# TensorE takes eight of the first sixteen modulation sums, and x goes to the head of the load queue

## The chip, the core and the metric

One core of a Trainium2 chip runs the whole program. Its engines are TensorE (PE in the rows; its weight loads PEld), VectorE (DVE), ScalarE (ACT), GpSimd (POOL) and SyncE (SP), each with a queue of its own that is worked off in order, and 16 DMA engines, which the queues of SP, ACT and POOL feed. The metric is the device time of one execution in microseconds.

## The reference

Two blocks on x of 256 tokens by 1024 features, in float32. The first has a gated delta-rule layer and a forgetting-attention layer, the second sliding-window attention, pooling, and a mixture that gathers expert rows. The change lies at the head of the first layer:

```python
cond = jax.nn.silu(c)
for i in range(DEPTH):
    mod = cond @ ada_w[i] + ada_b[i]
    shift, scale, gate = jnp.split(mod[:, None, :], 3, axis=-1)
    h = rmsnorm(x, norm_w[i]) * (1 + scale) + shift
    y = gdn_mixer(h, ...)            # i = 0: starts with proj = h @ w_in
    x = x + gate * y
```

Here `mod` has 3072 values a layer: 24 tiles of 128, where tiles 0 to 7 are the shift, 8 to 15 the scale and 16 to 23 the gate.

## The kernel before

Features lie on the 128 partitions in chunks of 128, so h is eight chunks of 128 by 256 tokens. `fm_steps` (L499 to L514) makes two chunks at a time: four transposes of the normed x (`xhat`) into a PSUM tile, then for each chunk ScalarE's pass (L511, with the modulation's scale `msc` and shift `mod` as columns) into the high part, VectorE's same pass (L512) into `xw`, and a difference (L513) for the low part. The matmuls of the dense layers take weights as high and low parts too, in three products of 256 columns (`dense_all`).

A modulation tile t is summed on VectorE (`ada`, L597 to L606): a row tile `raw` of 128 by 1024 weights, 512 KB, is loaded on SP's queue, multiplied with `silc` (silu of c, on every partition) and summed along the row (L604) into column t of `mod`. `rawp` has four `raw` buffers, and weights use them as well, so a load waits until the sum that read its buffer is done. `first` lists the sixteen tiles that h needs, pairs of scale and shift; `more(4)` issues four. `mod_scale` (L614) adds the bias and forms `msc` for two chunks a step, as soon as its four tiles are summed.

The order at the start is the code's order as the framework's scheduler keeps it on each engine: c, four row tiles, then x (L662), the identity and the small columns `pcol` on SP's queue; ScalarE squares x, `rstd` (L462 to L480) makes its norm by thirteen small VectorE steps, ScalarE writes `xhat` (L672), TensorE transposes. Between the third and fourth `fm_steps` stand ten dummy matmuls each (`WARM`, L688 to L690). The transfers share eight semaphores in turn, so each waits for the one eight before it.

Weights come in units: 512 KB of a matrix, loaded by `load` (L312) and taken apart by `cast` (L327 on ScalarE, L328 on VectorE), or used whole in f32 (`whole`). Units 0 and 1 are the first halves of the first two q and k columns, units 2 and 3 their second halves, used whole; unit 4 begins the next pair. `unit` hands out a unit in the order of `plan` and casts ahead. `gates` (through `small_proj`) needs all eight chunks as well, in products of 32 weight columns. From there on matmuls of all kinds follow one another to the expert part, whose gathers on GpSimd's queue fill the last half of the program.

Of the kernel before, what the change touches and what calls it, by code (L numbers as in the profile page):

```python
# [22 lines left out]
T = 256  # L23
D = 1024
# [39 lines left out]
for _n, _w in (("nw", 16), ("ab", 48), ("conv", 128), ("qn", 1), ("kn", 1), ("bq", 8),  # L64
               ("bk", 1), ("bga", 8), ("bgp", 8), ("ps", 4), ("anw", 1)):
    PO[_n] = _o
    _o += _w
# [47 lines left out]
def _pc(v, n):  # L115
    return np.ascontiguousarray(v.reshape(n, 128).T)


def prepare(a):
# [13 lines left out]
        _pc(b2[gp2:], 8), _pc(a["pool_scale_2"][0], 4),  # L133
        _pc(a["a_norm_w"][0], 1)], axis=1)
# [3 lines left out]
    ada = np.concatenate([a["ada_w"][0].T, a["ada_w"][1].T]).reshape(48, 128, D).transpose(1, 0, 2)  # L138
    sk = a["sub_keys_2"][0].transpose(3, 0, 1, 2).reshape(128, 16 * 128)
# [71 lines left out]
def build(nc, tc, ctx, I, out, dbg=None, stop=None):  # L211
# [8 lines left out]
    def transpose(o, i, e):  # L220
        M.t += math.prod(o.shape[1:]) * 2 / 2.4
        nc.tensor.transpose(o, i, e)  # L222

# [77 lines left out]
    raws, spare = {}, []  # L301
    trickle = [iter(())]

# [158 lines left out]
    def rstd(ss, n, e, name):  # L462
# [9 lines left out]
        for _ in range(3):  # L472
            if w == 1:
                V.tensor_scalar(z, y, y, x, op0=OP.mult, op1=OP.mult)
                V.tensor_scalar(y, z, 1.5, y, op0=OP.add, op1=OP.mult)
            else:
                V.tensor_tensor(z, y, y, op=OP.mult)
                V.tensor_tensor(z, z, x, op=OP.mult)
                V.scalar_tensor_tensor(y, z, 1.5, y, op0=OP.add, op1=OP.mult)
        return y  # L480
# [17 lines left out]

    def fm_steps(hi, lo, src, scale, bias, whole):  # L499

        for k0 in range(0, 8, 2):
            p = pss.tile([128, 2, T], F32, name="ps")
            for k in range(2):
                for b in range(2):
                    transpose(p[:, k, b * 128:(b + 1) * 128],
                                        src[b][:, (k0 + k) * 128:(k0 + k + 1) * 128], ident)
            v = whole[:, k0 % 4:k0 % 4 + 2]
# [86 lines left out]
    V.scalar_tensor_tensor(silc, silc, 1.0, c_row, op0=OP.add, op1=OP.mult)  # L594
    mod = cst.tile([128, 48], F32, name="mod")
    ada_done, ada_last = set(), []

    def ada(ts):

        for t in ts:  # L600
            w = rawp.tile([128, KU * CW], F32, name="raw", bufs=RAW_BUFS)
            nc.sync.dma_start(w, I["ada"][:, t, :])
            jk = act.tile([128, D], BF, name="jk", bufs=1)
            i = V.scalar_tensor_tensor(jk, w, 0.5, silc, op0=OP.mult, op1=OP.mult, accum_out=mod[:, t:t + 1])  # L604
            ada_last.append(i.ins)
            ada_done.add(t)  # L606
            yield

    def mod_cols(t, n):
# [44 lines left out]

    first = ada(t + 8 * i for t in range(8) for i in (1, 0))

    def more(n):
        for _ in range(n):
            next(first)

    more(4)
    nc.sync.dma_start(xs, I["x"].rearrange("(b p) d -> p b d", b=2))  # L662
    nc.sync.dma_start(const[:, 0:128], I["const"][:, 0:128])
    nc.sync.dma_start(pcol, I["pcol"])
    more(4)
    ssp = sums(1)
# [4 lines left out]
    for b in range(2):  # L671
        A.activation(xh0[b], xs[:, b], AF.Copy, scale=r0[:, b:b + 1])  # L672
    hi, lo = fm_tiles()
# [3 lines left out]
    hx = lambda kt: (hi[:, kt], lo[:, kt]) + ((xw[:, kt - 4],) if kt > 3 else ())  # L677
    next(ms)
    next(fm)
    more(4)  # L680
    next(ms)
    next(fm)
    cast(2, ahead=0)
    more(4)
# [1032 lines left out]
```

## Time and profile before

| | |
|---|---|
| median of 3 runs | 1396.33 us (1393.62 to 1399.25) |
| the profiled execution | 1398.01 us, its span 1396.2 us |
| busy: PE, DVE, ACT, POOL | 1233.9, 1017.3, 558.6, 306.5 us |
| mean granted clock of TensorE | 0.972 of full |
| chain that ended last, by engine | PE 49%, DMA 28%, DVE 12% |

The span runs from the first instruction to the last; 1.8 us of the execution lie outside it. A row of the timeline gives start and length in microseconds, the engine, the source line, and the operation as output<-inputs; x3 means that three alike follow one another, and the brackets hold the idle time ahead and what ended it. A matmul's record is longer than its step to the next one, since they overlap in the array. An f32 product that is not split is two records.

### The profile page before, as it was taken

What the parts mean: (1) busy time and instruction counts of PE and PEld (TensorE: products, weight loads), DVE (VectorE), ACT (ScalarE), POOL (GpSimd) and SP (SyncE); (2) the same over time, 40 slices, a digit from 0 to 9 for tenths busy, and PEclk for the clock granted to TensorE, in tenths of its full rate; (3) what the DMA queues carried; (4) which work ended last, traced back from release to release, by engine and by line L of the source; (5) the groups of instructions that cost most, each with busy time, mean ns of one, the idle gap of its engine ahead of it and who ended that gap; (6) DMA issues with size and microseconds to landing.
All of it is one profiled execution on the core that took longest, in us unless ns stands there. A gap on an engine that the chain in (4) does not pass through costs nothing.

```text
span 1396.2 us, 20024 instructions
## 1 busy us (share of the span) xinstructions
PE 1233.9 (88%) x6880; PEld 887.5 (64%) x6880; DVE 1017.3 (73%) x2670; ACT 558.6 (40%) x1313; POOL 306.5 (22%) x295
## 2 busy tenths in 40 slices
PE   1999999999899999999999999887778787877886
PEld 1888988989899988889986565333333333323332
DVE  6799988987876688775547657766777766767655
ACT  3357656574455555674213223222222221222211
POOL 0000000000000000000014434444343534444452
PEclk9999999999999999999999999999999989999899
DMA  8656464733454525335849999999999999999996
GB/s 302 200 159 203 137 182 138 224 93 120 123 171 146 167 85 197 116 98 173 278 178 421 423 389 366 423 425 422 424 424 424 412 424 424 419 420 427 404 423 254
DMA packets 72085, 392.39 MB, mean 281 GB/s; under 512 B 8112, under 2 KB 8624, under 8 KB 39472
## 3 DMA queue, kind: packets, MB, share of 16 engines
q0 software_dynamic: 37296, 268.45, 46.4%
q1 hardware_dynamic: 32960, 117.41, 26.5%
q10 hardware_dynamic: 1728, 5.24, 1.0%
q8 instruction: 55, 0.90, 0.3%
q14 instruction: 46, 0.38, 0.1%
HBM read 390.03 MB, written 1.05 MB: 280 GB/s over the span
## 4 chain that ended last, share of the span: by engine, by line
PE 49%; DMA 28%; DVE 12%; issue 5%; POOL 3%; ACT 2%; SPq 0%; POOLq 0%; DVEq 0%; ACTq 0%
PE pd L218 29%; DMA er<-uv,idx 22%; PE pacc L218 7%; PE ps L218 6%; DVE jk L1625 3%; POOL er L1622 3%; DMA raw<-awi 3%; PE ip L218 2%; DVE lo L328 2%; PE acc L218 2%; DMA er<-uv,i 1%; PE po L218 1%; PE ps L222 1%; DMA raw<-ada 1%; DVE jk L604 1%
## 5 line engine op out<-in xcount | busy, mean ns | idle before, releaser
L218 PE MATMUL pacc<-er,dg 128*128 128x512 f32 x1024 | 489.0, 631 | 106.8 <-ACT dg L1635 104.4
L1622 POOL DMA_INDIRECT er<-uv,idx x253 | 285.0, 1127 | 778.8 <-DVE oh L1572 427.6
L218 PEld LDWEIGHTS pacc<-er,dg 128*128 128x128 f32 x1024 | 200.0, 201 | 379.1 <-issue 220.7
L1625 DVE SCALAR_TENSOR_TENSOR jk<-er,xn 128x1024 bf16<-128x1024 f32 x256 | 312.4, 1220 | 151.1 <-DMA er<-uv,idx 150.2
L328 DVE TENSOR_TENSOR lo<-raw,hi 128x1024 fp32r<-128x1024 f32 x122 | 148.6, 1221 | 55.9 <-ACT hi L327 55.1
L1629 ACT ACTIVATE ge<-dots,r 128x2 f32<-128x2 f32 (+2 forms) x95 | 28.0, 295 | 384.9 <-DVE jk L1625 384.9
L327 ACT ACTIVATE hi<-raw 128x1024 fp32r<-128x1024 f32 x122 | 129.3, 1060 | 131.0 <-PE pd L218 82.8
L218 PE MATMUL pd<-fm,hi 128*128 128x256 f32 x784 | 153.4, 292 | 3.5 <-ACT hi L327 3.3
L218 PEld LDWEIGHTS pd<-fm,hi 128*128 128x128 f32 x784 | 123.6, 192 | 5.2 <-ACT hi L327 3.7
L218 PE MATMUL pd<-hi,fm 128*128 128x256 f32 (+1 forms) x608 | 117.3, 289 | 2.1 <-DVE fm L496 1.3
L218 PE MATMUL pd<-fm,lo 128*128 128x256 f32 x392 | 112.6, 287 | 0.0
L1635 ACT ACTIVATE dg<-const,ge 128x128 f32<-128x128 f32 x250 | 83.0, 391 | 37.3 <-DVE ge L1631 33.4
L218 PEld LDWEIGHTS pd<-hi,fm 128*128 128x128 f32 x608 | 95.5, 192 | 3.8 <-issue 2.3
L218 PE MATMUL pd<-lo,fm 128*128 128x256 f32 (+1 forms) x304 | 86.8, 287 | 1.6 <-DVE lo L328 1.6
L218 PEld LDWEIGHTS pd<-fm,lo 128*128 128x128 f32 x392 | 75.1, 192 | 0.2 <-issue 0.2
L218 PE MATMUL pd<-xw,raw 128*128 128x256 f32 x256 | 68.0, 391 | 2.9 <-DVE xw L512 1.7
L604 DVE SCALAR_TENSOR_TENSOR jk<-raw,silc 128x1024 bf16<-128x1024 f32 x48 | 58.5, 1219 | 2.9 <-DMA raw<-ada 2.6
L218 PEld LDWEIGHTS pd<-lo,fm 128*128 128x128 f32 x304 | 58.1, 192 | 2.0 <-DVE lo L328 2.0
L827 POOL TENSOR_SCALAR_AFFINE_SELECT am<-am 128x256 f32<-128x256 f32 x16 | 6.5, 406 | 213.0 <-DVE am L825 201.1
L873 ACT ACTIVATE is<-acc 128x256 f16<-128x256 f32 x96 | 36.9, 385 | 30.6 <-PE acc L218 28.7
L218 PEld LDWEIGHTS pd<-xw,raw 128*128 128x128 f32 x256 | 44.5, 193 | 7.0 <-DVE xw L512 2.0
L879 DVE TENSOR_TENSOR iy<-ip,fac 128x256 f16<-128x256 f32 x96 | 40.4, 420 | 9.0 <-PE ip L218 7.5
(393 smaller groups left out, 2151.9 us busy)
## 6 DMA issues: line engine op xcount, KB each, us to landing
raw<-ada SPq DMA_DIRECT2D x48, 512.0 KB, 4.4
raw<-awi SPq DMA_DIRECT2D x48, 512.0 KB, 4.1
raw<-bwi SPq DMA_DIRECT2D x32, 512.0 KB, 3.6
raw<-wi SPq DMA_DIRECT2D x30, 512.0 KB, 3.5
raw<-awo SPq DMA_DIRECT2D x16, 512.0 KB, 3.6
raw<-wqy SPq DMA_DIRECT2D x14, 512.0 KB, 7.7
raw<-bwo SPq DMA_DIRECT2D x8, 512.0 KB, 3.7
raw<-wau SPq DMA_DIRECT2D x8, 512.0 KB, 3.6
```

The source lines that it names most:

```text
L218: nc.tensor.matmul(o, l, r, **kw)
L222: nc.tensor.transpose(o, i, e)
L327: A.activation(hi, r3, AF.Copy)
L328: V.tensor_tensor(lo, r3, f(hi), op=OP.subtract)
L604: i = V.scalar_tensor_tensor(jk, w, 0.5, silc, op0=OP.mult, op1=OP.mult, accum_out=mod[:, t:t + 1])
L827: G.affine_select(am, am, pattern=[[0, 2], [1, 128]], base=0, channel_multiplier=-1, compare_op=OP.not_equal, fill=1.0)
L873: A.activation(s[:, 0:2], acc[:, 0:2], AF.Copy)
L879: V.tensor_tensor(y, p, bc2(FH[f"m{m}"]), op=OP.mult)
L1622: G.indirect_dma_start(out=r, out_offset=None, in_=I["uv"], in_offset=bass.IndirectOffsetOnAxis(ap=idx[:, b, h, s + i:s + i + 1], axis=0))
L1625: at["dot"] = V.scalar_tensor_tensor(jk, r[:, 0:D], 1.0, xn[:, b], op0=OP.mult, op1=OP.mult, accum_out=dots[:, i:i + 1]).ins
L1629: A.activation(ge, dots, AF.Gelu, scale=r3[:, b:b + 1])
L1635: A.activation(dg, ident, AF.Copy, scale=ge[:, i:i + 1])
```

## The change

Eight of the sixteen tiles (`ADA_PE`: 4 to 7 of the shift, 12 to 15 of the scale) are stored the other way round on the host, with the contraction on the partitions, and TensorE sums each of them as eight products of one column (`ada_sums`): weights `aw` 128 by 128 in f32, moving operand `cc`, silu of c as eight columns, which come in with `pcol`. ScalarE copies two columns at a time from PSUM into `mod`. The tiles `aw` lie in six buffers that later hold other tiles and in two of the buffers for high and low parts; two more of these (`spare`) take the first two units' weights, so that all four `raw` buffers are left to the eight row tiles. c is loaded on ScalarE's queue, x heads SP's. The VectorE sums are held behind the last step of the norm (`rstd`), TensorE's second to fourth pair of sums behind the second chunk pair's transposes (`turn`), the copies behind `xhat`. The third and fourth `fm_steps` (`features`) are issued when units 0 and 1 are handed out. The dummy matmuls are gone.

```diff
+ADA_PE = [4, 5, 6, 7, 12, 13, 14, 15]
...
-    nc.sync.dma_start(c_row, row_ap("c", 1024))
+    nc.scalar.dma_start(c_row, row_ap("c", 1024))
...
+    nc.sync.dma_start(xs, I["x"].rearrange("(b p) d -> p b d", b=2))
+    nc.sync.dma_start(pcol, I["pcol"])
+    nc.sync.dma_start(const[:, 0:128], I["const"][:, 0:128])
...
+        if at["use"] < 3:
+            next(early[0])
...
+    A.activation(cc, col("cc", 8), AF.Tanh, scale=0.5)
+    V.scalar_tensor_tensor(cc, cc, 1.0, col("cc", 8), op0=OP.add, op1=OP.mult)
...
+    def ada_sums(t, tiles):
+
+        p = pss.tile([128, 2], F32, name="ps")
+        for i, w in enumerate(tiles):
+            for k in range(8):
+                mm(p[:, i:i + 1], w[:, k], cc[:, k:k + 1], start=k == 0, stop=k == 7)
+            ada_done.add(t + 8 * i)
+        with tc.issue_after(at["xhat"]):
+            A.activation(mod[:, t:t + 9:8], p, AF.Copy, scale=0.5)
...
+    aws, rws = {}, {}
+    for t in range(3):
+        if t < 2:
+            rws.update((u, ada_row(u)) for u in (8 + t, t))
+        aws[4 + t] = ada_load(4 + t, [t4("aw") for _ in range(2)])
+    aws[7] = ada_load(7, [wts.tile([128, D], F32, name="aw", tag=m, bufs=HL_BUFS) for m in ("hi", "lo")])
...
-    next(ms)
+    ada_sums(4, aws[4])
     next(fm)
-    more(4)
-    next(ms)
-    next(fm)
+    fm2 = fm_steps(hi, lo, xh0, msc[:, 0], mod[:, 0:8], xw, 2)
+    next(fm2)
+    for t in range(4):
+        for u in (8 + t, t):
+            with tc.issue_after(at["rstd"]):
+                ada_dot(u, rws[u] if u in rws else ada_row(u))
+        if t:
+            with tc.issue_after(at["turn"]):
+                ada_sums(4 + t, aws[4 + t])
+        if t % 2:
+            next(ms)
+            next((fm, fm2)[t // 2], None)
+    fm = fm_steps(hi, lo, xh0, msc[:, 0], mod[:, 0:8], xw, 4)
+    spare.extend(wts.tile([128, KU * CW], F32, name="raw", tag=m, bufs=HL_BUFS) for m in ("hi", "lo"))
     cast(2, ahead=0)
-    more(4)
-    for _ in range(2):
-        next(ms)
-        next(fm)
-        pw = pss.tile([128, 2, T], F32, name="ps")
-        for k in range(WARM):
-            mm(pw[:, 0], hi[:, 2, 0:128], hi[:, 3], start=True, stop=True)
+
+    def features():
+
+        for _ in range(2):
+            next(fm)
+            with tc.issue_after(ada_last[7]):
+                next(ms)
+                next(fm)
+            yield
+
+    early.append(features())
```

TensorE's order at the start of the program, before (`xhat` transposes into `ps`, `pd` the dense products, `ps<-fm` the dummies):

```order
L222 MATMUL ps<-const,xhat 128x128 x12
L218 MATMUL pd<-fm,hi 128x256 x2
L218 MATMUL ps<-fm 128x256 x10
L218 MATMUL pd<-fm,lo 128x256
L222 MATMUL ps<-const,xhat 128x128 x4
L218 MATMUL ps<-fm 128x256 x10
L218 MATMUL pd<-fm,hi 128x256 x2
```

The same place now, with the one-column sums from the tiles `aw`:

```order
L221 MATMUL ps<-cc,aw 128x1 x16
L225 MATMUL ps<-const,xhat 128x128 x8
L221 MATMUL ps<-cc,aw 128x1 x40
L225 MATMUL ps<-const,xhat 128x128 x4
L221 MATMUL ps<-cc,aw 128x1 x8
L225 MATMUL ps<-const,xhat 128x128 x4
L221 MATMUL pd<-fm,hi 128x256 x2
```

All 64 sums stand ahead of the first dense product, 16 of them ahead of the first transpose.

ScalarE's order at the same place, before (`jka` squares x, `fm` is a feature pass, `hi` a unit's cast):

```order
L485 ACTIVATE jka,ssp<-xs 128x1024 x2
L672 ACTIVATE xhat<-xs,n_137 128x1024 x2
L511 ACTIVATE fm<-ps,mod,msc 128x256 x3
L327 ACTIVATE hi<-raw 128x1024
L511 ACTIVATE fm<-ps,mod,msc 128x256
L327 ACTIVATE hi<-raw 128x1024
L511 ACTIVATE fm<-ps,mod,msc 128x256 x2
```

And now, where `mod<-ps` is the copy of two summed columns out of PSUM:

```order
L701 ACTIVATE xhat<-xs,n_132 128x1024 x2
L641 ACTIVATE mod<-ps 128x2
L520 ACTIVATE fm<-ps,mod,msc 128x256
L641 ACTIVATE mod<-ps 128x2
L520 ACTIVATE fm<-ps,mod,msc 128x256
L641 ACTIVATE mod<-ps 128x2 x2
L520 ACTIVATE fm<-ps,mod,msc 128x256
L333 ACTIVATE hi<-raw 128x1024
L520 ACTIVATE fm<-ps,mod,msc 128x256 x3
```

The fourth copy, that of the last pair of sums, has come to stand ahead of the third and fourth chunk's passes and ahead of the first unit's cast.

## Rows read from the trace of the kernel before

**Rows 1.** Busy time by stage: microseconds and instructions of each engine, granted clock, DMA.

```profile
core 0: us, PE busy (x) PEld busy (x) DVE busy (x) ACT busy (x) POOL busy (x), PEclk, DMA share, GB/s
0.00:25.00 25.00, 0.33 (x2) 0.33 (x3) 14.52 (x44) 6.37 (x9) 0.20 (x4) 1.00 0.87 302
...
31.00:35.00 4.00, 3.80 (x18) 3.50 (x18) 3.24 (x5) 1.66 (x3) 0.00 (x0) 0.57 0.84 278
...
45.00:52.00 7.00, 5.96 (x25) 4.75 (x26) 3.67 (x6) 1.66 (x4) 0.00 (x0) 0.51 0.51 202
...
58.00:150.00 92.00, 91.26 (x727) 82.12 (x726) 85.19 (x221) 58.92 (x147) 5.71 (x14) 1.00 0.57 179
```

**Rows 2.** Timeline to 28 us: start, length, engine, line, instruction, idle before it.

```profile
3.65 0.61 SPq L662 DMA_DIRECT2D xs<-x  x1
...
14.66 1.06 ACT L485 ACTIVATE jka<-xs 128x1024 bf16<-128x1024 f32 x1 [7.31 <-DMA xs<-x]
...
17.02 0.17 DVE L467 TENSOR_SCALAR n<-ssp 128x2 f32<-128x2 f32 x1 [1.38 <-ACT jka L485]
...
23.28 0.16 DVE L479 SCALAR_TENSOR_TENSOR n<-n 128x2 f32<-128x2 f32 x1
...
23.47 2.19 ACT L672 ACTIVATE xhat<-xs,n 128x1024 f32<-128x1024 f32 x2 [6.48 <-DVE n L479]
...
24.67 3.22 PE L222 MATMUL ps<-const,xhat 128*128 128x128 f32 x12 [24.67 <-ACT xhat L672]
```

**Rows 3.** The same timeline, 30 to 58 us.

```profile
30.09 1.06 ACT L327 ACTIVATE hi<-raw 128x1024 fp32r<-128x1024 f32 x1 [1.11 <-DMA raw<-awi]
...
31.20 0.56 PE L218 MATMUL pd<-fm,hi 128*128 128x256 f32 x2 [3.31 <-ACT hi L327]
...
40.51 0.08 DVE L604 DVE_READ_ACCUMULATOR jk<-raw,silc 128x1 f32 x1
...
44.48 0.55 ACT L511 ACTIVATE fm<-ps,mod,msc 128x256 fp32r<-128x256 f32 x1
...
47.19 0.69 DVE L513 TENSOR_TENSOR fm<-xw,fm 128x512 fp32r<-128x512 f32 x1
...
57.74 0.59 PE L218 MATMUL pd<-fm,hi 128*128 128x256 f32 x2
```

**Rows 4.** Groups of instructions, 0 to 58 us: busy, mean ns, idle before.

```profile
L604 DVE SCALAR_TENSOR_TENSOR jk<-raw,silc 128x1024 bf16<-128x1024 f32 x16 | 19.5, 1221 | 0.9 <-DMA raw<-ada 0.8
...
L512 DVE TENSOR_SCALAR xw<-ps,msc,mod 128x256 f32<-128x256 f32 x8 | 4.2, 538 | 0.3 <-ACT fm L511 0.3
L328 DVE TENSOR_TENSOR lo<-raw,hi 128x1024 fp32r<-128x1024 f32 x3 | 3.7, 1225 | 3.3 <-ACT hi L327 3.3
...
L218 PE MATMUL ps<-fm 128*128 128x256 f32 x20 | 3.9, 361 | 0.0
```

**Rows 5.** Timeline again: products of few columns, and ten weight loads at either clock.

```profile
31.20 0.30 PEld L218 LDWEIGHTS pd<-fm,hi 128*128 128x128 f32 x2 [3.71 <-ACT hi L327]
31.65 2.21 PEld L218 LDWEIGHTS ps<-fm 128*128 128x128 f32 x10 [0.16 <-ACT fm L511]
...
34.91 1.26 PEld L218 LDWEIGHTS ps<-fm 128*128 128x128 f32 x10
...
67.63 0.62 PE L218 MATMUL ps<-g_tm,const 128*128 128x32 f32 x4 [0.35 <-DVE g_tm L726]
68.09 0.46 PE L218 MATMUL pd<-xw,raw 128*128 128x256 f32 x1
```

**Rows 6.** DMA bandwidth in 40 slices of 1.5 us, 0 to 60 us.

```profile
GB/s 0 157 233 303 371 407 412 426 396 423 423 391 107 235 183 328 369 287 314 300 336 322 208 292 210 191 292 141 161 397 423 371 137 11 0 188 161 218 131 96
```

**Rows 7.** Timeline, TensorE: three-product matmuls (256 columns) and whole f32 ones.

```profile
58.28 0.40 PE L218 MATMUL pd<-fm,hi 128*128 128x256 f32 x2
...
58.63 0.40 PE L218 MATMUL pd<-fm,hi 128*128 128x256 f32 x2
...
60.80 3.62 PE L218 MATMUL pd<-xw,raw 128*128 128x256 f32 x16
```

More of the change, by code (lines that the diff above doesn't have):

```diff
@@ L133, in prepare @@
         _pc(b2[gp2:], 8), _pc(a["pool_scale_2"][0], 4),
-        _pc(a["a_norm_w"][0], 1)], axis=1)
+        _pc(a["a_norm_w"][0], 1), _pc(a["c"][0], 8)], axis=1)
     row = np.concatenate([
@@ L137, in prepare @@
         b2[v2:ga2], a["final_norm_w"], a["ln_mix_g_2"][0], a["ln_ffn_g_2"][0], a["ln_final_g_2"]])[None]
-    ada = np.concatenate([a["ada_w"][0].T, a["ada_w"][1].T]).reshape(48, 128, D).transpose(1, 0, 2)
+    ada = np.concatenate([a["ada_w"][0].T, a["ada_w"][1].T]).reshape(48, 128, D).transpose(1, 0, 2).copy()
+    tiles = a["ada_w"][0].reshape(8, 128, 24, 128).transpose(1, 2, 0, 3).reshape(128, 24, D)
+    ada[:, ADA_PE] = tiles[:, ADA_PE]
     sk = a["sub_keys_2"][0].transpose(3, 0, 1, 2).reshape(128, 16 * 128)
@@ L221, in transpose @@
         M.t += math.prod(o.shape[1:]) * 2 / 2.4
-        nc.tensor.transpose(o, i, e)
+        return nc.tensor.transpose(o, i, e).ins
     V, A, G = nc.vector, nc.scalar, nc.gpsimd
@@ L301, in build @@
     raws, spare = {}, []
-    trickle = [iter(())]
+    trickle, early = [iter(())], []
     def load(upto):
@@ L478, in rstd @@
                 V.tensor_tensor(z, z, x, op=OP.mult)
-                V.scalar_tensor_tensor(y, z, 1.5, y, op0=OP.add, op1=OP.mult)
+                at["rstd"] = V.scalar_tensor_tensor(y, z, 1.5, y, op0=OP.add, op1=OP.mult).ins
         return y
@@ L497, in split, with fm_steps @@
         return V.tensor_tensor(lo, v, f(hi), op=OP.subtract)
-    def fm_steps(hi, lo, src, scale, bias, whole):
-        for k0 in range(0, 8, 2):
+    def fm_steps(hi, lo, src, scale, bias, whole, k1=0):
+        for k0 in range(k1, 8, 2):
             p = pss.tile([128, 2, T], F32, name="ps")
@@ L504, in fm_steps @@
                 for b in range(2):
-                    transpose(p[:, k, b * 128:(b + 1) * 128],
-                                        src[b][:, (k0 + k) * 128:(k0 + k + 1) * 128], ident)
+                    at["turn"] = transpose(p[:, k, b * 128:(b + 1) * 128],
+                                           src[b][:, (k0 + k) * 128:(k0 + k + 1) * 128], ident)
+            yield
             v = whole[:, k0 % 4:k0 % 4 + 2]
@@ L595, in build, with ada_row, ada_dot, ada_load @@
     mod = cst.tile([128, 48], F32, name="mod")
+    cc = cst.tile([128, 8], F32, name="cc")
+    A.activation(cc, col("cc", 8), AF.Tanh, scale=0.5)
+    V.scalar_tensor_tensor(cc, cc, 1.0, col("cc", 8), op0=OP.add, op1=OP.mult)
     ada_done, ada_last = set(), []
+    def ada_row(t):
+        assert t not in ADA_PE
+        w = rawp.tile([128, KU * CW], F32, name="raw", bufs=RAW_BUFS)
+        nc.sync.dma_start(w, I["ada"][:, t, :])
+        return w
+    def ada_dot(t, w):
+        jk = act.tile([128, D], BF, name="jk", bufs=1)
+        i = V.scalar_tensor_tensor(jk, w, 0.5, silc, op0=OP.mult, op1=OP.mult, accum_out=mod[:, t:t + 1])
+        ada_last.append(i.ins)
+        ada_done.add(t)
     def ada(ts):
         for t in ts:
[L601 to L606, printed above, removed]
-            yield
+            ada_dot(t, ada_row(t))
+            yield
+    def ada_load(t, tiles):
+        for i, w in enumerate(tiles):
+            nc.sync.dma_start(w, I["ada"][:, t + 8 * i, :])
+        return [w.rearrange("p (k c) -> p k c", k=8) for w in tiles]
+    def ada_sums(t, tiles):
+        p = pss.tile([128, 2], F32, name="ps")
+        for i, w in enumerate(tiles):
+            for k in range(8):
[3 more added lines that the diff above has]
+            A.activation(mod[:, t:t + 9:8], p, AF.Copy, scale=0.5)
     def mod_cols(t, n):
@@ L653, in add_gated_block @@
         return xs[:, b, cs]
[L655 to L659, printed above, removed]
-    more(4)
-    nc.sync.dma_start(xs, I["x"].rearrange("(b p) d -> p b d", b=2))
-    nc.sync.dma_start(const[:, 0:128], I["const"][:, 0:128])
-    nc.sync.dma_start(pcol, I["pcol"])
-    more(4)
+    aws, rws = {}, {}
[4 more added lines that the diff above has]
+    aws[7] = ada_load(7, [wts.tile([128, D], F32, name="aw", tag=m, bufs=HL_BUFS) for m in ("hi", "lo")])
     ssp = sums(1)
@@ L671, in build @@
     for b in range(2):
-        A.activation(xh0[b], xs[:, b], AF.Copy, scale=r0[:, b:b + 1])
+        at["xhat"] = A.activation(xh0[b], xs[:, b], AF.Copy, scale=r0[:, b:b + 1]).ins
     hi, lo = fm_tiles()
```

5 lines of the change are left out of this document (2 added, 3 removed).

## The prediction

> **What bounds the kernel now.** I read the table of busy time by stage first [rows 1]. TensorE is busy 91.3 of 92 us between 58 and 150 us, so whatever starts the matmuls after 58 us sooner should end the program sooner by as much; there is nothing in that stretch for a delay to hide in. The last two thirds of the program wait for gathers that follow from the same work and move along with it. The room is ahead of 58 us: TensorE does 0.33 us of work in the first 25 us, and in two later stretches the granted clock is 0.57 and 0.51, near the lower of its two levels (1.2 GHz). So the question is at what time the dense work of the first two pairs of units is over. Before, that is 57.74 us, where the matmuls of the fifth unit begin [rows 3].
>
> The timeline of the start tells why [rows 2]. x is issued sixth on SP's queue and its square waits for it until 14.66 us. The norm's small steps run on VectorE from 17.02 to 23.44 us, because the modulation sums (1.22 us each, [rows 4]) stand between them; four of them fit in there, some 4.9 us of the 6.4. Only then come xhat (23.47) and the transposes (24.67). Unit 0's cast waits for its weights until 30.09, the first dense pair comes at 31.20, and the last features are done at 47.88 (47.19 + 0.69), behind the sixteenth sum (40.51) [rows 3].
>
> **x and the norm first.** Up to x the queue carried 3.85 MB before and carries about 1.75 MB now (crow, the small transfers and x). The row of bandwidths [rows 6], added up slice by slice, has moved 3.85 MB by 13.0 us, and x was there at 14.64, so 1.6 us later; 1.75 MB are moved by 7.9 us, which puts x at about 9.4 us. Two squares take 2.4 us (14.66 to 17.02, [rows 2]), the norm without the sums 1.5 to 2.6 us. xhat starts at about 14.3 us, 9 us sooner. Nothing of that is a gain by itself: what comes next is late for other reasons.
>
> **Transfers.** From there on 524 kB take 1.27 us at the 412 GB/s of the busiest slices [rows 6]. Nothing starves: there are now eight more buffers ahead of the waits on VectorE, where before SP waited for a sum before each load. The order of SP's queue gives the first tile for TensorE (behind x, pcol, ident and two rows) at 13.7 us, each transfer 1.27 us behind the one before, the eighth TensorE tile at 25.2, the last VectorE row at 30.3, unit 0's weights at 31.5 and unit 1's, queued behind a load that waits for a VectorE sum, at 35.5. Before, unit 0's cast began at 30.09, so the weights themselves come 1.4 us later, not sooner.
>
> **The sums on TensorE.** VectorE loses 8 of its 16 sums, 8 x 1.30 = 10.4 us with their read-outs. TensorE gets 64 products of one column with 128x128 f32 weights. Such a product is two records, as the 32-column and 16-column ones are: four records from 67.63 to 68.09 us, 0.115 us each, with hardly any columns to stream [rows 5]. So what costs is the weight load. The ten loads of [rows 5] take 2.21 us at the lower level and 1.26 us at the higher: a load goes with the clock, 0.21 against 0.11 us or a little more. The price of 64 sums is then 128 x 0.112 = 14.3 us at 2.4 GHz and 128 x 0.215 = 27.5 us at 1.2 GHz. A tile is 1.8 or 3.4 us, against the 1.27 us between two landings, so TensorE and not the memory sets the end of the sums. With 64 sums, 16 transposes (8 ahead of the last 48 sums, 4 more ahead of the last 8) and three waits of about 0.5 us for ScalarE to copy a pair of sums out of the one PSUM buffer that they share, the last sum ends at
>
> - higher level reached within the first pair: 13.7 + 5.3 + 3 x 3.6 + 12 x 0.11 + 1.5 = 32.6, say 33 us;
> - lower level throughout: 13.7 + 4 x 6.9 + 12 x 0.215 + 1.5 = 45.4, say 45 us.
>
> **What hangs on the last sum.** The order of ScalarE shows it: the last copy of a pair of sums stands ahead of the features of the third and fourth chunk and ahead of unit 0's cast. ScalarE is in order, so unit 0 waits for the last sum although its weights are there at 31.5. Behind the copy (0.3 us) I add by the rows of the same steps [rows 3, 4]: a feature pass 0.56, unit 0's cast 1.06, its low part 1.22, then VectorE's two passes, one difference, a mask's cast, two more passes, a difference (0.5, 0.5, 0.65, 0.4, 0.5, 0.55, 0.6) until unit 1's low part, 1.2: about 8 us in all. TensorE works beside that on unit 0 and the gates' projection. After it some 28 of the 72 matmuls of 0.12 us are left (three in 0.36 us, [rows 7]), 3.4 us, and the sixteen whole products: 32 records of 0.226 us, 7.25 us [rows 7]. With 0.3 us for the small transposes that is 19 us from the last sum to the fifth unit.
>
> **Sum.** At the higher level 33 + 19 = 52 us against 57.74: 5.7 us gained. The 20 warm-up matmuls are gone (3.9 us of records, [rows 4]); they lay in waits and cost nothing, but without them the clock may fall while TensorE waits for casts at 33 to 41 us, which would take back 0 to 2 us. I take 5 us. The profiled execution was 1398.0 us (span 1396.2 and 1.8 outside it), 1.7 us over the median of the three runs; 5 us off the median, 1396.33, is 1391.3. Unknown ends: the sums from 1.8 to 3.4 us a tile, the bandwidth 5% either way (1.2 us at 30 us).
>
> **Does a stream of weight loads raise the clock?** The whole sign hangs on that, and no row of before has one-column products in a row. The nearest rows speak for it, weakly. The twelve transposes from 24.67 [rows 2] ran at the lower level's pace (about 0.21 us apart), and the two loads at 31.20 stand 0.30 us long for the pair, where the full-level stretch at 34.91 shows 1.26 us for ten [rows 5]: the clock had risen behind transposes that are half weight load. (The column of granted clock reads 1.00 there from the start, so it can't be trusted ahead of that.) It rose again after 3.7 us of matmuls, 31.2 to 34.9, but in the stretch 45 to 52 us only after some 6 us of work that filled the engine [rows 1].
>
> The Trainium skill's page "TensorE: Matmul & The Clock Gate" (section "Part 4: PE-mode transpose") says that transpose mode does not count as work for the gate and leaves the clock down. The loads at 31.20 differ from that. By that page sums that are nearly all weight load would hardly count either, and the time would be that of the first rival. The same page's "LDWEIGHTS" section prices a load by its columns alone, without the clock (an estimate of 107 ns for 128); the two rows of ten loads differ, so the measurement decides and the price at the lower level stands.
>
> **Rivals.**
> 1. The clock stays down through the sums (slower). For it: hardly a column streams, and the sums keep TensorE from the 256-column matmuls that raised the clock before. Against it: the transposes above. Last sum at 45, fifth unit at 45 + 19 = 64 us and up to 2 us more for a cold start of the dense work: 6.3 to 8.5 us lost, 1403.7 us. It decides from the point where the last sum ends after 57.7 - 19 = 38.7 us, that is above 0.16 us for a record.
> 2. TensorE is quicker than I price it, and the memory sets the end. Then the last VectorE row (30.3, its sum to 31.5, columns to 32.1) starts the same chain in place of the copy at 33.3: 1.2 us sooner, and the clock doesn't fall: 7 us gained, up to 8.5 with 426 GB/s; 1389.
> 3. The change does not bring what it says: x, norm and sums are early, but unit 0 and unit 1, whose weights come later than before and are cast late in ScalarE's queue, hold the dense work, and TensorE runs it at the lower level. Weights at 35.5 with a cast and a low part behind five feature steps, 72 matmuls of 0.21 us in place of 0.12: the fifth unit at 56 to 58 us, 1395.5 us.
>
> **How the numbers follow.** Forecast 0.42, rival 1 0.29, rival 2 0.15, rival 3 0.14. Half a per cent, about what a measurement can tell from no change here, is 7 us: below 1389.3 or above 1403.3. The forecast spreads over 1388 to 1394.5 and gives 0.10 to faster and the rest to same; rival 2 gives 0.12 to faster; rival 1, 1401 to 1406, gives 0.17 to slower and 0.12 to same; rival 3 is same. So faster 0.22, same 0.61, slower 0.17. The range leaves out about 0.1 at each end: 1387 to 1404.5. Gains hold most of the chance; the forecast's own range is 1388 to 1394.5.
>
> **What would show it.** x's square near 9.4 us, xhat near 14.3, the first sum near 13.7. The records of the sums: 0.11 us apart and a granted clock near 1.0 from about 19 us (forecast), or 0.21 and 0.5 (rival 1). The end of the last sum, 33 or 45 us, with unit 0's cast right behind the copy in both. The fifth unit's matmuls near 52 us, not 57.7. From there the two traces should run parallel to the end; if they don't, what I took for a fixed rest is not one. The forecast is wrong if the last sum ends after 38.7 us, if weights land later than 31.5 and hold the cast, or if the gain at the fifth unit is lost again by 150 us.

## The result: 15 us slower, and the profile after

The changed kernel takes 1411.47 us (median of five runs, 1408.79 to 1415.29), the kernel before 1396.36 (five runs): a ratio of 1.0109, 95% interval [1.0094, 1.0123], 15.1 us or 1.1% slower. The profiled execution of the changed kernel spans 1409.7 us, that of before 1396.2. The forecast (1391.3 us) and its range (to 1404.5) are both missed.

The start first. TensorE's timeline of the changed kernel (start, length, engine, line, instruction; in brackets the wait ahead of it) answers to [rows 2, 3, 5]:

```profile
12.78 6.96 PE L221 MATMUL ps<-cc,aw 128*128 128x1 f32 x32 [12.78 <-DVE n L486]
19.60 1.95 PE L225 MATMUL ps<-const,xhat 128*128 128x128 f32 x8
21.34 6.83 PE L221 MATMUL ps<-cc,aw 128*128 128x1 f32 x32
28.43 6.99 PE L221 MATMUL ps<-cc,aw 128*128 128x1 f32 x32 [0.26 <-ACT mod L641]
35.68 3.57 PE L221 MATMUL ps<-cc,aw 128*128 128x1 f32 x16 [0.26 <-ACT mod L641]
39.11 1.09 PE L225 MATMUL ps<-const,xhat 128*128 128x128 f32 x4
40.00 3.41 PE L221 MATMUL ps<-cc,aw 128*128 128x1 f32 x16
43.67 1.11 PE L225 MATMUL ps<-const,xhat 128*128 128x128 f32 x4 [0.26 <-ACT mod L641]
45.07 0.79 PE L221 MATMUL pd<-fm,hi 128*128 128x256 f32 x2 [0.28 <-ACT hi L333]
...
63.58 0.59 PE L221 MATMUL pd<-fm,hi 128*128 128x256 f32 x2
```

The 32 records of the first pair take 6.82 us from their start to the next group (12.78 to 19.60), 0.213 us each, and all later pairs the same: the sums run at the lower level's pace from the first to the last, which ends at 43.41. The last row is the start of the fifth unit, 5.8 us later than in [rows 3]. ScalarE's timeline of the same kernel shows what hung on the sums:

```profile
8.17 1.06 ACT L493 ACTIVATE jka<-xs 128x1024 bf16<-128x1024 f32 x1 [0.25 <-DMA xs<-x]
...
12.90 2.19 ACT L701 ACTIVATE xhat<-xs,n 128x1024 f32<-128x1024 f32 x2 [2.40 <-DVE n L487]
...
28.20 0.17 ACT L641 ACTIVATE mod<-ps 128x2 f32<-128x2 f32 x1 [6.69 <-PE ps L221]
...
35.45 0.17 ACT L641 ACTIVATE mod<-ps 128x2 f32<-128x2 f32 x1 [6.62 <-PE ps L221]
43.45 0.17 ACT L641 ACTIVATE mod<-ps 128x2 f32<-128x2 f32 x1 [7.82 <-PE ps L221]
43.51 0.56 ACT L520 ACTIVATE fm<-ps,mod,msc 128x256 fp32r<-128x256 f32 x1
43.96 1.05 ACT L333 ACTIVATE hi<-raw 128x1024 fp32r<-128x1024 f32 x1
```

x's square starts at 8.17 us (14.66 in [rows 2]) and xhat at 12.90 (23.47), and then ScalarE stands in front of the copies for 6 to 8 us each. Unit 0's cast comes at 43.96, right behind the last one.

The fifth unit is 5.8 us late, but the program ends 13.5 us late. VectorE's timeline at two later places, before and then after, shows that the distance has grown to 8.4 us by the next stage and is 8.0 when the gathers begin to set the pace; the last third adds 5.5 more:

```profile
394.97 0.18 DVE L1084 TENSOR_TENSOR fx<-ps,small 128x32 f32<-128x32 f32 x1
...
872.24 0.17 DVE L1576 SCALAR_TENSOR_TENSOR idx<-ei 128x16 uint32<-128x16 f32 x1
```

```profile
403.37 0.18 DVE L1128 TENSOR_TENSOR fx<-ps,small 128x32 f32<-128x32 f32 x1
...
880.23 0.17 DVE L1620 SCALAR_TENSOR_TENSOR idx<-ei 128x16 uint32<-128x16 f32 x1
```

For the stretch behind the fifth unit I take 290 us from its start on, in the table of busy time, before and after:

```profile
57.74:347.74 290.00, 285.10 (x2389) 259.58 (x2388) 257.74 (x688) 178.17 (x441) 12.88 (x32) 1.00 0.51 157
```

```profile
63.58:353.58 290.00, 282.19 (x2369) 256.23 (x2368) 253.59 (x665) 177.28 (x440) 13.26 (x32) 1.00 0.48 155
```

TensorE (the first pair behind the length) stands idle 4.9 us before and 7.8 after. For the gathers the row of their queue between 900 and 1300 us holds packets, MB and the share of the 16 engines' time; before and after:

```profile
q0 software_dynamic: 23100, 168.21, 100.6%
```

```profile
q0 software_dynamic: 22791, 165.98, 100.4%
```

The engines are full in both, yet fewer packets go through. Share x 16 x 400 us / packets gives 278.7 ns a packet before and 281.9 after: 1.1% more, on the path that sets the end for the last 500 us.

So there are three losses at three places, and I had priced only the first, as rival 1. The experiments took them apart.

### The profile page after: what moved, and what is told of

Same layout as the page of the kernel before. It is cut to its first block, busy times and chain, and to the rows that moved or that the text cites. A ratio compares the mean times of both kernels' runs of the same rounds, so it can differ in the third digit from the quotient of the medians.

```text
span 1409.7 us, 20222 instructions
## 1 busy us (share of the span) xinstructions
PE 1258.4 (89%) x6988; PEld 912.4 (65%) x6988; DVE 1011.2 (72%) x2655; ACT 559.5 (40%) x1318; POOL 311.8 (22%) x295
## 4 chain that ended last, share of the span: by engine, by line
PE 48%; DMA 26%; DVE 13%; issue 7%; POOL 4%; ACT 2%; POOLq 0%; DVEq 0%; ACTq 0%
PE pd L221 27%; DMA er<-uv,idx 21%; PE ps L221 8%; PE pacc L221 6%; POOL er L1666 4%; DVE jk L1669 3%; DVE lo L334 2%; DMA raw<-awi 2%; PE ip L221 2%; PE acc L221 2%; PE ps L225 1%; PE po L221 1%; DMA er<-uv,i 1%; DMA raw<-ada 1%; PE pt L225 1%
## 5 line engine op out<-in xcount | busy, mean ns | idle before, releaser
L1666 POOL DMA_INDIRECT er<-uv,idx x253 | 289.5, 1144 | 782.6 <-DVE oh L1616 428.5
L618 DVE SCALAR_TENSOR_TENSOR jk<-raw,silc 128x1024 bf16<-128x1024 f32 x40 | 48.8, 1219 | 3.8 <-DMA raw<-ada 3.6
```

The lines of the kernel that those rows point to most:

```text
L1666: G.indirect_dma_start(out=r, out_offset=None, in_=I["uv"], in_offset=bass.IndirectOffsetOnAxis(ap=idx[:, b, h, s + i:s + i + 1], axis=0))
```

## The experiments

All ratios are to the kernel before, run beside each kernel on the same chip (its medians there were 1396.4 beside the changed kernel and 1397.4 to 1398.2 beside the others). The ratios are of medians; the other columns are read from one profiled execution each. "Fifth unit" is the start of its matmuls, "last sum" its end on whichever engine has it, "idle" TensorE's idle time in the 290 us from there, "packet" the ns of a gather's packet as worked out above.

| kernel | ratio [95%] | last sum | fifth unit | idle | packet |
|---|---|---|---|---|---|
| before (as profiled) | 1 | 40.6 | 57.74 | 4.9 | 278.7 |
| changed | 1.0109 [1.0094, 1.0123] | 43.4 | 63.58 | 7.8 | 281.9 |
| b_pad_sbuf | 1.0039 [1.0025, 1.0053] | 40.7 | 53.96 | 5.9 | 281.6 |
| b_pad_dram | 0.9992 [0.9983, 1.0001] | 39.2 | 56.18 | 6.1 | 279.3 |
| b_off256 | 0.9993 [0.9981, 1.0005] | 38.8 | 56.41 | 5.0 | 278.7 |
| b_rows_a | 0.9966 [0.9951, 0.9982] | 39.5 | 53.34 | 4.5 | 276.9 |
| a_align | 1.0069 [1.0054, 1.0085] | 43.3 | 62.87 | 10.2 | 278.9 |
| a_nosums | 1.0024 [1.0014, 1.0035] | 31.0 | 51.95 | 8.2 | 281.2 |
| a_mix | 1.0142 [1.0127, 1.0156] | 48.9 | 67.97 | 9.2 | 281.6 |
| a_warm | 1.0107 [1.0088, 1.0125] | 41.1 | 61.37 | 9.0 | 280.8 |
| a_pe0_align | 1.0066 [1.0050, 1.0082] | 36.4 | 55.13 | 6.9 | 281.6 |
| a_pe4_align | 1.0047 [1.0029, 1.0066] | 38.1 | 58.67 | 7.5 | 278.9 |
| a_pe4b_all | 0.9971 [0.9962, 0.9980] | 31.7 | 51.21 | 8.4 | 277.8 |
| a_gates | 0.9950 [0.9937, 0.9964] | 31.6 | 52.10 | 5.8 | 276.5 |

### The sums on TensorE

**a_nosums**: one product of eight.

```diff
-            for k in range(8):
-                mm(p[:, i:i + 1], w[:, k], cc[:, k:k + 1], start=k == 0, stop=k == 7)
+            mm(p[:, i:i + 1], w[:, 0], cc[:, 0:1], start=True, stop=True)
```

> The changed kernel with one of the eight products of each tile on TensorE, 8 products in place of 64; the other seven eighths of these sums are left out, and the transfers stay. Theory: the sums' weight loads at the lower clock (0.213 us a record, 128 records) hold the last copy, and with it unit 0's cast. Without them the last of these sums follows its tile's landing (about 25 us in place of 43.4), the next limit is unit 0's and unit 1's weights and VectorE's last sums, and the fifth unit starts at 51 to 54 us in place of 63.6; the end comes 9.5 to 12.5 us sooner than in the changed kernel, 1399 to 1402 us. Rival: the queue of casts behind late weights and the lower clock hold the dense work anyway. Then the fifth unit starts at 57 us or later and the end is not below 1404.

The time is 1401.1 us, the fifth unit starts at 51.95: both as the theory has them. The 56 products that are missing are worth 11.6 us at the fifth unit (63.58 to 51.95). TensorE's timeline shows the sums following the landings, as they were meant to:

```profile
20.61 0.56 PE L221 MATMUL ps<-cc,aw 128*128 128x1 f32 x2 [0.78 <-DMA aw<-ada]
21.80 0.59 PE L221 MATMUL ps<-cc,aw 128*128 128x1 f32 x2 [0.63 <-DMA aw<-ada]
...
24.59 0.42 PE L221 MATMUL ps<-cc,aw 128*128 128x1 f32 x2
```

**a_mix** and **a_warm**: wide matmuls that nobody reads, to raise the clock. a_warm has only the last part of this diff.

```diff
                 mm(p[:, i:i + 1], w[:, k], cc[:, k:k + 1], start=k == 0, stop=k == 7)
+                if k % 4 == 3:
+                    mm(pw[:, 0], xs[:, 0, 0:128], xs[:, 0, 0:T], start=True, stop=True)
...
+    pw = pss.tile([128, 2, T], F32, name="ps")
+    for _ in range(WARM):
+        mm(pw[:, 0], xs[:, 0, 0:128], xs[:, 0, 0:T], start=True, stop=True)
     ada_sums(4, aws[4])
```

> The changed kernel with ten unused f32 matmuls of 256 columns on x ahead of the first sums, while TensorE has nothing to do, and one more behind every fourth product of the sums (16). Theory: the one-column products don't raise the clock, and wide matmuls do. Then from about 15 us on the sums' records are 0.11 us apart in place of 0.213, a tile takes 1.8 us and two dummies of 0.45; with 14.3 us of loads, 7.2 of dummies, transposes and copies the last sum ends at 36 to 38 us, the fifth unit starts at 56 to 58 us, 6 to 7 us sooner, and the end is at 1405 us. Rival: a 128x128 f32 load takes 0.21 us in such a row whatever the clock (it waits for the one-column product, not for the clock). Then the dummies add 7 us or more to the sums, the fifth unit starts at 70 us or later and the end is at 1418 us.

Neither: 1417.46 us and a fifth unit at 67.97, close to the rival, yet the rival's reason is wrong too. TensorE's timeline of a_mix:

```profile
8.03 6.11 PE L221 MATMUL ps<-xs 128*128 128x256 f32 x20 [8.03 <-DMA xs<-x]
13.98 0.95 PE L221 MATMUL ps<-cc,aw 128*128 128x1 f32 x8
14.79 0.68 PE L221 MATMUL ps<-xs 128*128 128x256 f32 x2
...
22.17 2.77 PE L221 MATMUL ps<-xs 128*128 128x256 f32 x6
24.73 3.72 PE L221 MATMUL ps<-cc,aw 128*128 128x1 f32 x32
28.32 1.20 PE L221 MATMUL ps<-xs 128*128 128x256 f32 x2
```

Right behind the wide matmuls eight records take 0.81 us (13.98 to 14.79), and 32 records 3.59 (24.73 to 28.32): 0.10 to 0.11 us each. So a load does go with the clock, as the prediction had it. But the higher level doesn't last. The granted clock reads 0.50 from 18 to 24 us, although two of every ten records ahead of that are wide ones; 0.90 between 24 and 28, behind six wide ones in a row; 0.53 between 28 and 32, behind 32 sums in a row; and 0.50 up to 52, again with two wide ones in ten. TensorE has no pause in all that time.

> The changed kernel with only the ten unused f32 matmuls of 256 columns on x ahead of the first sums, and none among them (where they stood among the sums as well, the records of the sums were 0.10 us apart right behind the ten, then the granted clock read 0.50 from 18 us to 24 and from 28 to 50, and the sums ended at 49). Theory A: TensorE is at the higher level when the sums begin and keeps it, since the sums themselves use it little; records 0.11 us apart to the end, the last sum at 31 to 33 us, the fifth unit at 51 to 53, the end at 1401 us. Theory B: the one-column products can't hold the higher level; after the first few microseconds the records go back to 0.21 us apart, the last sum ends at 40 to 43 us and the end is within 3 us of the changed kernel, 1409 to 1412.

Theory B, with 1412.31 us. TensorE's timeline of a_warm, and its table of busy time (the number behind POOL's pair is the granted clock):

```profile
8.29 7.36 PE L221 MATMUL ps<-xs 128*128 128x256 f32 x20 [8.29 <-DMA xs<-x]
15.49 3.63 PE L221 MATMUL ps<-cc,aw 128*128 128x1 f32 x32
...
19.89 6.01 PE L221 MATMUL ps<-cc,aw 128*128 128x1 f32 x32
26.16 6.98 PE L221 MATMUL ps<-cc,aw 128*128 128x1 f32 x32 [0.26 <-ACT mod L641]
```

```profile
18.00:20.00 2.00, 2.00 (x21) 2.00 (x20) 0.34 (x3) 0.41 (x2) 0.00 (x0) 1.00 1.02 408
20.00:22.00 2.00, 2.00 (x16) 2.00 (x14) 0.54 (x1) 0.33 (x1) 0.00 (x0) 0.69 1.03 412
22.00:24.00 2.00, 2.00 (x11) 2.00 (x11) 0.00 (x0) 0.00 (x0) 0.00 (x0) 0.50 1.02 408
```

The first pair takes 3.49 us (15.49 to 18.98, 0.109 a record), the second slows down on its way, the third is back at the changed kernel's pace (6.98 us, there 6.99), and the column falls from 1.00 to 0.50 while TensorE is busy all of the time. Here the one-column sums neither raise the clock nor hold it. Starting them at the higher level brings the last sum 2.3 us forward, no more. Why the level falls under them the records don't say; that stays open.

### The last third: where the row buffers lie

**b_pad_sbuf**: the kernel before with 64 more bytes a partition in the constants' pool, as many as the change adds. **b_pad_dram**: the kernel before with a wider pcol in DRAM alone.

```diff
     small = cst.tile([128, 64], F32, name="small")
+    gap = cst.tile([128, 16], F32, name="gap")
+    nc.vector.memset(gap, 0.0)
```

```diff
-        _pc(a["a_norm_w"][0], 1)], axis=1)
+        _pc(a["a_norm_w"][0], 1), np.zeros((128, 8), np.float32)], axis=1)
...
-    nc.sync.dma_start(pcol, I["pcol"])
+    nc.sync.dma_start(pcol, I["pcol"][:, 0:NPCOL])
```

> The kernel before, with nothing changed but 64 unused bytes a partition in the pool of constants (as many as the change adds there with its wider pcol and its cc), which move later buffers up, four of the ten buffers of the gathered rows among them. The question is the last 500 us: between 340 and 880 us the changed kernel runs a steady 8.0 to 8.4 us behind, but it ends 13.5 us behind, and the gathers of that stretch move 420 GB/s where they moved 424. Theory A: the gathers are slower because the row buffers lie 64 bytes further on. Then this kernel loses the same 5 to 6 us: 1402 us (1400 to 1404), 420 GB/s from 950 to 1250 us. Theory B: it is the place of the table in DRAM, which the 4 KB more of pcol moved. Then nothing changes here: 1396.4 us within 2, and 424 GB/s. Theory C: the tail is slower because the work reaches it in another order. Then nothing changes in either of the two padded kernels.

> The kernel before, with nothing changed but eight unused columns (4 KB) at the end of pcol in DRAM, which the kernel doesn't load; SBUF is laid out as before. Theory A (row buffers in SBUF moved by 64 bytes): no change, 1396.4 us within 2, gathers at 424 GB/s. Theory B (the table of rows moved by 4 KB in DRAM): 1402 us (1400 to 1404), 420 GB/s from 950 to 1250 us. Theory C (order of the work): no change.

Theory A in both: 1403.81 us, 5.5 us slower, with SBUF moved, and 1397.69, no change, with DRAM moved. The queue's rows, b_pad_sbuf and then b_pad_dram:

```profile
q0 software_dynamic: 22819, 166.16, 100.4%
```

```profile
q0 software_dynamic: 22986, 167.39, 100.3%
```

281.6 and 279.3 ns a packet. 64 bytes in front of everything, with no instruction added to the long loops, cost as much as a third of the whole loss.

**a_align**: the changed kernel with four buffers put back on the multiple. **b_off256**: the kernel before with the same four moved by 256 bytes. Both add one unused tile ahead of them, of 112 or 64 columns:

```diff
     ws.close()
+    gb = ctx.enter_context(tc.tile_pool(name="gap_b", bufs=1)).tile([128, 112], F32, name="gap_b")
+    V.memset(gb[:, 0:1], 0.0)
     rows_p.append(ctx.enter_context(tc.tile_pool(name="rows_b", bufs=1, reuse_waits="tile")))
```

> The changed kernel with 448 unused bytes a partition right ahead of the four row buffers that the change moved by 64 bytes, so that they lie on a multiple of 512 bytes again, as in the kernel before; nothing else differs. Theory: the place of these buffers is 5 to 6 us of the 15, and what is left (9 to 10 us) is lost ahead of 340 us. Then 1405.5 to 1407.5 us, with gathers back at 424 GB/s between 950 and 1250 us. Rival: in the changed kernel the gathers are slower for another reason as well, such as the place of the table in DRAM. Then it stays above 1409.

> The kernel before with 256 unused bytes ahead of the four row buffers that lie on a multiple of 512 bytes; they then lie on an odd multiple of 256. Theory A: what matters is a multiple of 512. Then this costs what 64 bytes cost, 5 to 6 us: 1402 to 1404 where before is at 1397. Theory B: a smaller multiple is enough, and 64 bytes off cost because 64 is too small. Then it is within 2 us of before.

a_align takes 1407.47 us, a ratio of 1.0069 in place of 1.0109, so 5.6 us come back: about the same price from the other side. b_off256 is unchanged at 1396.83: theory B, 256 bytes off cost nothing.

**b_rows_a**: the other six buffers of the kernel before, which lie 32 bytes off, put on the multiple as well.

```diff
+    ga = ctx.enter_context(tc.tile_pool(name="gap_a", bufs=1, side="right")).tile([128, 8], F32, name="gap_a")
+    V.memset(ga[:, 0:1], 0.0)
     rows_p = [ctx.enter_context(tc.tile_pool(name="rows_a", bufs=1, side="right", reuse_waits="tile"))]
```

> The kernel before with 32 unused bytes a partition ahead of the other six row buffers, which lie 32 bytes off a multiple of 512; with that all ten lie on one. Theory A: a gather into a buffer off the multiple costs more whatever the distance; four buffers at 64 bytes off cost 5.6 us, so six at 32 off would cost 8.5, and this kernel gains that: 1388 to 1391 us. Theory B: only the four buffers, or only an offset that isn't 32, matter. Then it is within 2 us of before.

1392.98 us: 4.7 us faster than before, with 276.9 ns a packet. Theory A in kind, but not in size: 0.8 us for a buffer 32 bytes off, where 64 bytes off cost 1.4.

### Other ways to split the sums

**a_pe0_align**: no sums on TensorE (the row buffers lie 64 bytes off here, whatever the label says).

```diff
-ADA_PE = [4, 5, 6, 7, 12, 13, 14, 15]
+ADA_PE = []
...
```

Left out of the diff: the buffers `aw` take row tiles, and VectorE's loop runs over all sixteen.

> The changed kernel with none of the sums on TensorE: x, its norm and the transposes come first as in the change, the spare buffers stay, and VectorE makes all sixteen sums; the row buffers lie as in the changed kernel (64 bytes off). Theory: x and its norm first are worth some microseconds by themselves, and the sums on TensorE cost more than they bring. VectorE needs 16 times 1.30 us and some 3 us of feature steps from 12.9 us on, so the last sum is at 36 to 38 us, the fifth unit starts at 53 to 55 us (57.74 before, 63.6 in the changed kernel), and the end is 8 to 10 us ahead of the changed kernel, 1401 to 1404, of which 5.6 are the place of the row buffers. Rival: VectorE is the bound again, as it was before; the sixteen sums then hold the low parts of the first units as long as before, the fifth unit starts at 57 to 59 us and the end is at 1405 to 1408.

VectorE's last sum ends at 36.4 and the fifth unit starts at 55.13, as expected, but the time is 1406.09, 2 us above the range and within the rival's. Against the traces with the old start (fifth unit at 53.3 to 57.7) nothing is gained by x and its norm alone. VectorE has no pause from 12.8 us to the last sum there, and unit 1's cast waits for its weights until 40.68.

**a_pe4_align**: four tiles on TensorE and twelve sums on VectorE, and the four row buffers back on the multiple.

```diff
-ADA_PE = [4, 5, 6, 7, 12, 13, 14, 15]
+ADA_PE = [6, 7, 14, 15]
...
```

Left out of the diff: the order of the loads, VectorE's loop over twelve tiles, the place of the sums, and the unused tile of a_align.

> The changed kernel with four tiles on TensorE in place of eight and twelve sums on VectorE, and with the four row buffers on a multiple of 512 bytes. Theory: with 64 records of 0.213 us on TensorE (13.7 us from 12.8, and 8 transposes between) and 12 sums of 1.30 on VectorE both end at 29 to 32 us, about when unit 0's weights land (31.5); the fifth unit starts at 50.5 to 53 us, 5 to 7 us ahead of the kernel before, and the end is 2 to 5 us ahead of it, since the order of the work from 60 to 340 us that goes with the new start has cost 2.4 to 3.5 us in both kernels seen so far: 1393 to 1396 us where the kernel before is at 1398. Rival: the last copy on ScalarE holds unit 0's cast here too, or the dense work runs at the lower clock; then the fifth unit starts after 56 us and there is no gain.

The rival by its numbers (1405.4 us, fifth unit at 58.67), but the main reason is another: TensorE's last sum, though done at 28.1, holds VectorE. The second copy stands ahead of a feature pass in ScalarE's order, and a step of VectorE that needs this pass stands ahead of six of its sums. ScalarE's and VectorE's rows:

```profile
28.17 0.17 ACT L641 ACTIVATE mod<-ps 128x2 f32<-128x2 f32 x1 [6.69 <-PE ps L221]
```

```profile
28.83 0.55 DVE L521 TENSOR_SCALAR xw<-ps,msc,mod 128x256 f32<-128x256 f32 x1 [6.78 <-ACT fm L520]
```

VectorE stands for 6.8 us in the middle of its sums, and the last of them ends at 38.1 in place of some 31.

**a_pe4b_all**: the copies behind unit 0's cast, the first transposes ahead of the sums, all ten row buffers on the multiple. The diff is against a_pe4_align.

```diff
-            A.activation(hi, r3, AF.Copy)
+            at.setdefault("hi", A.activation(hi, r3, AF.Copy).ins)
...
+    def ada_copy(t, p):
+        with tc.issue_after(at["hi"]):
+            A.activation(mod[:, t:t + 9:8], p, AF.Copy, scale=0.5)
...
-    ada_sums(6, aws[6])
     next(fm)
...
     next(fm2)
+    with tc.issue_after(at["turn"]):
+        ps6, ps7 = ada_sums(6, aws[6]), ada_sums(7, aws[7])
...
```

> Four tiles on TensorE and twelve sums on VectorE as in the run with four tiles, but the transposes of the first four chunks stand ahead of the sums on TensorE, ScalarE copies the sums out only behind unit 0's cast (there, the second copy stood ahead of a feature pass in ScalarE's order and held VectorE idle for 6.8 us, from 21.9 to 28.8), and all ten row buffers lie on a multiple of 512 bytes. Theory: with VectorE never idle the last of its sums ends at 32 us in place of 38, unit 0's low part follows at about 33.5 to 35, the fifth unit starts at 51 to 54 us (58.7 there; 53.3 to 57.7 in four traces of the kernel before and its padded copies); the row buffers are worth 4.7 us, measured in the kernel before, and the end is 1388 to 1392 us where the kernel before is at 1397. Rival: the weights of units 0 and 1 (cast at 34 and 41 us in the runs seen) set the fifth unit and not the sums. Then it starts at 55 us or later and only the place of the row buffers is gained: 1392 to 1394.

The start is as the theory has it (last sum 31.7, fifth unit 51.21), the time is 1393.32, not below 1392: no better than the row buffers alone. The 4 us at the fifth unit are lost again, with TensorE idle 8.4 us behind it.

**a_gates**: the same with one edge moved.

```diff
...
-        with tc.issue_after(ada_last[-1]):
+        with tc.issue_after(los[2]):
             split(hi, lo, raw)
```

Here los[2] is the low part of the third unit.

> The kernel of the last run with four tiles (ten row buffers on a multiple of 512 bytes, 1393.3 us), with one edge moved: VectorE splits the gates' weights only behind the low part of the third unit, not right behind its last sum, so that the gates' projection and what hangs on it (g_tm, the row products) come on TensorE later than in the changed kernel's order and near where the kernel before had them. From the fifth unit to 290 us on, TensorE has stood idle 6.9 to 10.2 us in eight traces with the changed start and 4.5 to 6.1 us in five traces with the old one, which is where a start 4 us sooner has been lost. Theory: it is the gates coming early that makes the longer waits; put late, the idle time falls to 5 or 6 us and the end comes 2 to 3 us sooner, 1390 to 1391.5 where the kernel before is at 1397. Rival: the whole order of that stage is another one whatever the place of the gates, and a new order is a new draw; then the idle time is anywhere from 5 to 11 us and the end from 1390 to 1396.

1390.69 us, a ratio of 0.9950: faster than both kernels, 7.0 us ahead of before and, by the two ratios, 22 ahead of the changed one. But 4.7 of the 7.0 us are what b_rows_a gains by the place of the row buffers alone; the 2.3 that are left to the new start are hardly clear of the noise, since the intervals of b_rows_a and a_gates overlap between 0.9951 and 0.9964. The waits of TensorE behind the fifth unit, of a_pe4b_all, which differs by this edge alone, and of a_gates (us in total, times, longest):

```profile
PE ip L221 <- ACT is L929: 3.6, 5, 1.1
PE acc L221 <- DVE iy L950: 1.1, 1, 1.1
...
PE ip L221 <- ACT tf L942: 0.3, 1, 0.3
```

```profile
PE ip L221 <- ACT is L929: 2.1, 3, 1.2
...
PE ip L221 <- DVE iy L935: 0.2, 1, 0.2
PE acc L221 <- DVE iy L935: 0.2, 1, 0.2
```

The waits for the solver's steps (is, tf, iy) fall from 5.0 us to 2.5 (5.8 in the changed kernel), and the idle time from 8.4 us to 5.8. That is the theory's result, but it lies in the rival's range as well. Moving the gates moves much else in that stage, and it is a single order that was tried; that it is the gates' early coming that makes the waits is likely, not shown. What is shown is the other half: eight traces with the changed start stand idle 6.9 to 10.2 us there, five with the old one 4.5 to 6.1. (One trace alone says little: the changed kernel and a_align have the same order, and stand idle 7.8 and 10.2 us.)

## Why the prediction was wrong, point by point

**x and the norm first: right.** x's square at 8.17 us (9.4 predicted), xhat at 12.90 (14.3), the first sum at 12.78 (13.7): all about a microsecond sooner than reckoned.

**The price of a load: right at both levels.** 0.213 us a record at the lower (0.215 predicted) and 0.109 at the higher (0.112). It was read from loads that stand between products of 256 columns, which could have set that spacing too; only the one-column products show that it is the load's. The Trainium skill's page "TensorE: Matmul & The Clock Gate", section "LDWEIGHTS (loading the stationary operand)", prices a load by its columns alone, which is 107 ns for 128 of them (an estimate by its formula); the runs agree at the higher level and show double at the lower.

**The level: the step that failed.** The forecast had the clock rise within the first pair of sums, because in the trace of the kernel before it had risen behind twelve transposes [rows 5]. In the changed kernel it does not rise: 8 transposes at 19.60 and 4 at 39.11 stand among the sums, and the pace stays at 0.213 from the first sum to the last. The row that the forecast rested on was read rightly. The two loads at 31.20 were at the higher level: the pair takes 0.30 us, against 0.50 for the same pair in the changed kernel. Until then TensorE had done nothing but the twelve transposes, and the column of granted clock (behind POOL's pair), whose 1.00 tells nothing ahead of its first change, shows the fall right behind these loads:

```profile
28.00:31.00 3.00, 0.00 (x0) 0.00 (x0) 3.00 (x6) 1.47 (x2) 0.00 (x0) 1.00 0.96 325
31.00:32.00 1.00, 0.80 (x3) 0.65 (x4) 0.85 (x2) 0.60 (x2) 0.00 (x0) 0.76 0.94 303
32.00:33.00 1.00, 1.00 (x6) 1.00 (x6) 0.86 (x2) 0.62 (x1) 0.00 (x0) 0.50 0.85 332
```

But that was one execution. The four padded copies of the kernel before start with the same twelve transposes, and in none of them is the first dense pair at the higher level: its loads take 0.50 us for the pair (b_pad_dram, b_off256) or stand apart with 0.29 us each (b_pad_sbuf, b_rows_a). The pair of products, 0.56 us at 31.20 [rows 3], in b_pad_dram:

```profile
29.90 0.79 PE L218 MATMUL pd<-fm,hi 128*128 128x256 f32 x2 [2.75 <-ACT hi L327]
```

So the step took for a rule what one trace of five shows, and carried it from transposes to one-column products, of which no row of before has a run; in no trace here did a run of them raise the clock. Why the one trace differs stays open. The same page's section "Part 4: PE-mode transpose" has transposes leave the clock down: four of the five traces agree, the one in [rows 5] doesn't. That section says nothing of one-column products; to carry it over to them was my own step, and there the runs bear it out. With the break-even at 0.16 us a record, the level alone turns the sign of the forecast. Rival 1 had it, and its steps hold: last sum at 43.4 (45 predicted), 20.2 us from there to the fifth unit (19), fifth unit at 63.58 (64).

**The granted clock as the judge: wrong.** I wrote that the column would read near 0.5 in rival 1. It reads 1.00 from the start to 90 us in the changed kernel, over records 0.213 apart; only the spacing told the level. In a_warm and a_mix, where the column changes early, it agrees with the spacing from then on.

**"From there the two traces should run parallel": wrong, and worth half of the loss.** Two terms were missing in the sum of every case, so that even rival 1, right up to the fifth unit, came out at 1403.7, 7.8 us short. a_nosums shows it without the level in the way: its fifth unit starts at 51.95, where the forecast had it (52), and its end is 1401.1 us, not 1391.3.

- The row buffers: the diff adds 32 bytes to pcol and 32 for cc in a pool that lies ahead of nearly everything. I costed their transfer and never asked what they push. They cost 5.5 us (b_pad_sbuf), and 5.6 come back (a_align).
- The order of the stage behind the fifth unit: 7.8 us of idle time on TensorE against 5.3, the mean of the five traces with the old start; 2.5 us. The order of that stage is made anew from the changed start, which I had taken for a fixed rest.

**The mark of 57.74 us was itself late.** The four padded copies of the kernel before, whose start is the same but for a `memset` in b_pad_sbuf, reach the fifth unit at 53.34 to 56.41; the mean of the five is 55.5. They differ by the clock: between 46 and 49 us it reads 0.50 in before, b_pad_dram and b_off256, which reach the fifth unit at 56.18 to 57.74, and 1.00 in b_pad_sbuf and b_rows_a, at 53.96 and 53.34. So a start of this kernel that is read from one trace is good to some 2 us either way. Measured from the mean, the changed start loses 8.1 us. 8.1 + 2.5 + 5.5 = 16.1 us, against 15.1 measured (13.1 to 17.2); the first two terms are of single traces, and the fit is no closer than that.

**Rivals 2 and 3.** The memory set nothing: only a_nosums followed the landings. Rival 3 (early steps that bring nothing, because the first units' weights and casts are late) comes near what a_pe0_align shows once the sums are back on VectorE.

## What to carry to other kernels

Read a clock's level from the spacing of many equal records, and look at the same place in several traces before taking it for a rule: here one of five had the level that the forecast rested on. Don't count on a kind of work to raise the clock that no row shows at the higher level. When a change adds bytes to a pool, ask which buffers lie behind it, and what address a transfer that sets the pace then writes to; 64 bytes cost 5.5 us here. A gain at the start is a gain at the end only if the order of the work behind it stays; with a scheduler between, compare the idle time of the next stage in several traces of each kernel before calling a difference of 3 us a cause.

## What the runs showed of the hardware

**Gathers depend on the byte at which their buffer starts.** With rows of 8 KB, a packet takes 276.5 to 277.8 ns when all ten buffers lie on a multiple of 512 bytes, 278.7 to 279.3 when four do and six lie 32 bytes off (also when those four lie on an odd multiple of 256), and 280.8 to 281.9 when the four lie 64 bytes off. Fourteen traces fall into these three groups without overlap. The Trainium skill's page "DMA: Bandwidth & Descriptors", section "How a descriptor splits into AXI transactions", says that a transfer is cut at multiples of 256 bytes and that a read which starts off them pays for a partial piece. The run at 256 bytes agrees with it, for writes into SBUF; the size doesn't. By that section 64 bytes are two beats more on 256, an estimate of 0.8%, and only for the four buffers; the packet over all ten rose by 0.9%, from the mean of the second group to that of the third.

**The granted clock can fall under a TensorE that has no pause.** In a_warm it went from 1.00 to 0.50 between 20 and 24 us, in the middle of 64 sums, with TensorE busy from 8.3 us on; in a_mix it fell twice, at 18 us with two wide records in ten and at 28 us behind 32 sums in a row. The stretch behind the fifth unit, where wide matmuls follow one another, reads 1.00 in both tables of 290 us above. The records show that the clock falls, and not why.
